# Opening a hybrid encoder layer with two column tiles interleaved, four tiles ahead of the first evacuation, and the gates' arithmetic spread among the matmuls

## The chip, the core and the metric

One NeuronCore of a Trainium2 chip runs the whole program in one launch. TensorE (PE, with its weight loads PEld), VectorE (DVE), ScalarE (ACT), GpSimd (POOL) and SyncE (SP, which only issues transfers here) each run their own queue in order and meet at semaphores. PE writes to PSUM, whose banks hold one 128x512 fp32 tile each; the other engines bring results from there to SBUF. The metric is the device time of one execution in microseconds, as the median of several runs.

## The reference

A layer on 512 tokens (two requests of 256) of width 2048, in fp32:

```python
xn = rmsnorm(h, norm_mix_w)
proj = xn @ w_in                       # 2048 x 7200
y_na = neighbourhood_attention(q, k, v, rpb)          # 8 heads of 128
qkv = silu(conv5(qkv)); q, k = l2norm(q), l2norm(k)   # 8 delta heads
beta = sigmoid(b)
g = -exp(A_log) * softplus(a + dt_bias)               # the gates
y_dn = delta_rule(q, k, v, g, beta) + flip(delta_rule(flipped ...))
h = h + concat(y_na, rmsnorm_and_silu_gate(y_dn, z)) @ w_out
h = h + (silu(rmsnorm(h) @ w_gate) * (rmsnorm(h) @ w_up)) @ w_down
y = rmsnorm(h, final_norm_w)
```

Within chunks of 64 tokens the delta rule needs the products k k^T and q k^T of each head (the "grams"), the running sum G of g, and the decays exp(G_c - G_s).

## The kernel before

Tokens lie along the free axis: x is held transposed, as 16 blocks (k-blocks) of 128 features by 512 tokens, and a *column tile* is 128 columns of `w_in` against all of them, accumulated in one PSUM bank. To keep fp32 precision every operand is split into a rounded high part and the rest (`split`, lines 134 to 142: ACT writes `hi`, DVE writes `lo`), and each k-block is three matmuls, hi hi, hi lo and lo hi (`mm3`). So a column tile is 48 matmuls. Its weights come in two halves of 512 KB (`load_w`), each from one of three SBUF buffers (`w_raw`, `w_hi`, `w_lo`); a buffer comes free when PE has used the half three before it.

The column tiles run in the order k0, q0, k1, q1, ... k7, q7 (key and query of each delta head), then the attention heads' q, k, v, then the rest. The RMS norm's per-token factor (`rstd`) isn't applied to x: each column tile is multiplied by it when it is evacuated from PSUM (`evac`, line 308). So the first evacuation waits for `token_rstd`: sixteen squares on ACT, their sum on DVE, a product with a matrix of ones on PE, a square root on ACT and four reciprocals on DVE.

The opening loads x and the two halves of k0 in quarters, in the order in which PE takes them (`load_k0`, `split_x`). Before its data are there, PE runs `WARM` products of a constant. After k0 come the 32 narrow products `ps_ba` for the gates' inputs a and b, then q0, the first half of k1, the ones product, the second half of k1, then q1. The column tiles take the three banks of the pool `pg` in turn; smaller products take the three banks of `psm` (`ps_s`).

For a delta head, `conv_silu` evacuates a tile (`ev_xi`), multiplies it with the five taps of the convolution (one on ACT, four on DVE, `cacc`), and applies silu on ACT into `kq`. Then ACT squares q (`q_sq`) and splits the squares (`sqh`, `sql`). `kq_post`, here called the head's post, makes the grams: eight gram products into two banks of `ps_s`, two products of the squares into the third, then copies by ACT (`gs`, line 380; `qrow`, line 388) and transfers by POOL. It runs as a generator: while PE's program is written, `pump` is called after every two k-blocks of a half tile (four times per half tile, eight per column tile), and each call advances the oldest post in `chains` and the oldest generator in `side` by one step. The first post fires at pump 21 (`KQ_START`), each later one 8 pumps after the post before it, or after it was put in the queue, whichever is later (`KQ_GAP`).

`gates` reads a and b back from DRAM with sixteen small transfers by POOL and computes softplus, g, G, beta and their exponentials on small tiles, called once after head 0. From head 2 on, `decays` puts 22 exponentials per head on ACT, in program order with the head's other ACT work (`pin`). Apart from what is pinned a scheduler orders each engine's instructions by priority; the weights' splits are raised by `AHEAD`.

Of the kernel before, what the change touches and what calls it, by code (L numbers as in the profile page):

```python
# [18 lines left out]
P = 128  # L19
T = 512  # L20
# [35 lines left out]
FIN_GAP = 5  # L56

LANE_WORK = 1800
OPEN_AT = 0
HALF, BAND = 32, 40  # L60

WARM = 56

DECAY_HEAD = 2
DECAY_ROWS = 11
# [2 lines left out]
def r32(ap):  # L68
    return ap.bitcast(F32)
# [3 lines left out]
def hybrid_encoder(ctx: ExitStack, tc: tile.TileContext, xT, w_in, w_ba, w_out, w_gate,  # L73
# [163 lines left out]
    def sm_tile():  # L237
        return psm.tile([P, T], F32, tag="s", name="ps_s")
# [8 lines left out]
    ba_raw = wp.tile([P, KT, 32], F32, tag="raw", bufs=3, name="ba_raw")  # L247
    baw = ini.tile([P, KT, 32], F32, tag="baw", name="ba_w")
    k0w = []

    def split_x(j):
        for i in range(2):
            k = 2 * j + i
            x, w = xr[j][:, i], nwm[:, k:k + 1]
            pin(act(out=xs[k][0], in_=x, func=AF.Copy, scale=w))
            stt(xs[k][1], x, w, r32(xs[k][0]), ALU.mult, ALU.subtract)  # L256


    ps = sm_tile()
# [2 lines left out]
        mm(ps[:, :2 * P], idle[:, :P], idle, start=True, stop=True)  # L262


    def load_k0(i, k):
        if k == 0:
            k0w.append((wp.tile([P, 8, P], F32R, tag="hi", bufs=3, name="w_hi"),
                        wp.tile([P, 8, P], F32R, tag="lo", bufs=3, name="w_lo"),
                        wp.tile([P, 8, P], F32, tag="raw", bufs=3, name="w_raw")))
        hi, lo, raw = [t[:, k:k + 4] for t in k0w[i]]  # L270
        nc.sync.dma_start(raw, w_in[0, i][:, k:k + 4])
        pin(act(out=hi, in_=raw, func=AF.Copy))
        tt(lo, raw, r32(hi), ALU.subtract)

    def load_x(j, i):
        nc.sync.dma_start(xr[j][:, i], xT[j][:, i])

    load_k0(0, 0)
    for j in range(8):
        if j == 0:  # L280
            load_x(0, 0)
            load_x(0, 1)
        else:
            nc.sync.dma_start(xr[j], xT[j])
        split_x(j)
        if j == 0:
            load_k0(0, 4)
        if j in (2, 4):
            load_k0(1, 2 * j - 4)
        if j == 5:  # L290
            nc.sync.dma_start(ba_raw, w_ba)
    tt(baw, ba_raw, nwm[:, :, None].broadcast_to([P, KT, 32]), ALU.mult)

    def token_rstd():
        acc = ini.tile([P, T], F32, tag="acc", name="ssq_acc")
        for k in range(KT):
            sq = acc if k == 0 else ini.tile([P, T], F32, tag="sq", bufs=2, name="x_sq")
            pin(act(out=sq, in_=xr[k // 2][:, k % 2], func=AF.Square))
            if k:
                tt(acc, acc, sq, ALU.add)  # L300
# [103 lines left out]
    def vec(nm, w=C):  # L404
        return ln.tile([P, w], F32, tag=nm, name=nm)
# [3 lines left out]
    def gates():  # L409
        bl, al = vec("bl", 4 * C), vec("al", 4 * C)  # L410
        for d in range(2):
            for t, r in ((bl, d * 8), (al, 16 + d * 8)):
                for k in range(4):
                    p0 = d * 64 + k * 16
                    nc.gpsimd.dma_start(
                        t[p0:p0 + 16].rearrange("p (g t) -> p g t", g=4),
                        s_ba[:, r:r + 8].rearrange("g h (b c t) -> (h b) g c t", b=NB, c=4)[:, :, k])
        for t in (bl, al):
            tt(t[:, :2 * C], t[:, :2 * C], t[:, 2 * C:], ALU.add)
            tt(t[:, :C], t[:, :C], t[:, C:2 * C], ALU.add)  # L420
# [3 lines left out]
        ts(xa, al, lpar[:, 0:1], None, ALU.add)  # L424
# [4 lines left out]
        ts(z, e, 2.0, None, ALU.add)  # L429
        nc.vector.reciprocal(z, z)  # L430
        tt(z, z, e, ALU.mult)
        tt(z2, z, z, ALU.mult)
        ts(sp, z2, 1.0 / 17, 1.0 / 15, ALU.mult, ALU.add)
# [3 lines left out]
        stt(sp, sp, 2.0, z, ALU.mult, ALU.mult)  # L437
        stt(sp, xa, 0.0, sp, ALU.max, ALU.add)
        g = vec("g")
        ts(g, sp, ea, -1.0, ALU.mult, ALU.mult)  # L440

        on = vec("on")
        nc.vector.memset(on, 1.0)  # L443
        G, NG = vec("G"), vec("NG")
        nc.vector.tensor_tensor_scan(G[half[0]], on[half[0]], g[half[0]], 0.0, ALU.mult, ALU.add)
        nc.vector.tensor_tensor_scan(G[half[1], ::-1], on[half[1]], g[half[1], ::-1], 0.0,
                                     ALU.mult, ALU.add)
# [3 lines left out]
        nc.vector.tensor_copy(tot[half[1]], G[half[1], 0:1])  # L451

        beta = vec("beta")
# [12 lines left out]
        nc.gpsimd.memset(E, 0.0)  # L466
        gt.update(G=G, NG=NG, beta=beta, kd=kd, eg=eg, dg=dg, E=E)
# [119 lines left out]

    for h in range(H):
        kq = wk.tile([P, 2, T], F32, tag="kq", bufs=2, name="kq")
        if h == 1:  # L590
            half_gemm(ps_k1, w_in[2, 1], xs[8:], False, True)
        ps = (ps_k0, ps_k1)[h] if h < 2 else col_tile(w_in[2 * h], xs)
        conv_silu(ps, 8 + h, kq[:, 0])
        ps = ps_q0 if h == 0 else col_tile(w_in[2 * h + 1], xs)
        conv_silu(ps, h, kq[:, 1])
        sq = na.tile([P, T], F32, tag="qT", name="q_sq")
        pin(act(out=sq, in_=kq[:, 1], func=AF.Square))
# [813 lines left out]
```

## Time and profile before

| | us |
|---|---|
| median of 3 runs | 2282.72 (2281.67 to 2284.06) |
| profiled execution | 2278.2 |
| its span in the trace | 2276.4 |
| PE busy | 2246.1 |
| DVE busy | 1768.7 |
| ACT busy | 1060.1 |
| POOL busy | 237.8 |

The span is the time from the first to the last instruction of the profiled execution. PE busy counts the matmuls, whose ends overlap the next ones' starts, so how fast PE advances is better read from the distance between starts. A wait is named by the instruction that waits and the one that released it.

### The profile page before, as it was taken

The page shows a single profiled execution, that of the slowest core. Times are in us where ns is not written, and L with a number is a line of the kernel's source. Part 1 is how long each engine was busy: PE and PEld are TensorE (multiplying, and loading weights), DVE is VectorE, ACT ScalarE, POOL GpSimd, SP SyncE. Part 2 cuts the span into 40 slices and gives each one's busy share as a digit, 9 for nine tenths or more (in the row PEclk, how much of TensorE's full clock was granted, in tenths as well). Part 3 has the DMA queues.
Part 4 walks back from the last instruction along what each step waited for, and adds up shares of the span by engine and source line. Part 5 has one row for each costly group of instructions (what it writes and reads, how often), then busy time and mean ns, then how long its engine had stood idle before and what let it go on. Part 6 is the DMA issues. An engine that isn't in the chain of part 4 may idle for free.

```text
span 2276.4 us, 32532 instructions
## 1 busy us (share of the span) xinstructions
PE 2246.1 (99%) x12318; PEld 1918.4 (84%) x12318; DVE 1768.7 (78%) x2691; ACT 1060.1 (47%) x1637; POOL 237.8 (10%) x343
## 2 busy tenths in 40 slices
PE   9999999999999999999999999999999999999998
PEld 7887778888888888888888888888888878888887
DVE  7654699984556546898888888888888788898966
ACT  6777332323333425654444444444444454444435
POOL 2211100010000011111111110111100011011010
PEclk9999999999999999999999999999999999999999
DMA  5333422254333455677777777777777477667672
GB/s 203 128 124 128 132 94 96 95 134 143 107 103 102 185 176 173 214 196 208 199 199 198 199 215 198 211 200 204 201 197 191 149 200 201 177 191 212 177 204 84
DMA packets 112828, 383.95 MB, mean 169 GB/s; under 512 B 14080, under 2 KB 14416, under 8 KB 112416
## 3 DMA queue, kind: packets, MB, share of 16 engines
q1 hardware_dynamic: 77264, 267.17, 34.2%
q0 software_dynamic: 34256, 112.61, 23.3%
q8 instruction: 97, 1.59, 0.3%
q10 hardware_dynamic: 1152, 2.10, 0.2%
q14 instruction: 59, 0.48, 0.1%
HBM read 346.41 MB, written 35.41 MB: 168 GB/s over the span
## 4 chain that ended last, share of the span: by engine, by line
PE 80%; DVE 10%; ACT 4%; issue 3%; DMA 2%; POOL 0%; SPq 0%; DVEq 0%; ACTq 0%; POOLq 0%
PE ps_g L85 25%; PE ps_c L85 14%; PE ps_d L85 14%; PE ps_a L85 14%; PE ps_b L85 7%; PE ps_s L85 5%; DVE w_lo L137 2%; DVE W L566 2%; DVE prod L564 1%; ACT w_hi L136 1%; DVE cacc L352 1%; ACT E L473 1%; ACT E L475 1%; PE ps_o L85 1%; DMA kkq<-s_gram 1%
## 5 line engine op out<-in xcount | busy, mean ns | idle before, releaser
L85 PE MATMUL ps_g<-xhi,w_hi 128*128 128x512 f32 x896 | 358.1, 400 | 1.6 <-DVE on L443 1.4
L85 PE MATMUL ps_g<-xhi,w_lo 128*128 128x512 f32 x896 | 350.4, 391 | 3.1 <-DVE w_lo L137 3.1
L85 PE MATMUL ps_g<-xlo,w_hi 128*128 128x512 f32 x896 | 349.6, 390 | 0.5 <-DVE xlo L256 0.5
L137 DVE TENSOR_TENSOR w_lo<-w_raw,w_hi 128x1024 fp32r<-128x1024 f32 x166 | 202.6, 1222 | 137.0 <-ACT w_hi L136 136.3
L136 ACT ACTIVATE w_hi<-b 128x1024 fp32r<-128x1024 f32 (+1 forms) x180 | 185.7, 1032 | 236.4 <-issue 119.0
L136 ACT ACTIVATE w_hi<-w_raw 128x1024 fp32r<-128x1024 f32 x166 | 174.6, 1056 | 243.3 <-PE ps_g L85 197.2
L136 ACT ACTIVATE w_hi<-w_first 128x1024 fp32r<-128x1024 f32 (+1 forms) x180 | 185.3, 1029 | 186.4 <-PE ps_c L85 90.3
L137 DVE TENSOR_TENSOR w_lo<-w_first,w_hi 128x1024 fp32r<-128x1024 f32 (+1 forms) x180 | 213.7, 1187 | 65.0 <-ACT w_hi L136 58.7
L137 DVE TENSOR_TENSOR w_lo<-b,w_hi 128x1024 fp32r<-128x1024 f32 (+1 forms) x180 | 212.9, 1183 | 7.1 <-ACT w_hi L136 6.7
L85 PEld LDWEIGHTS ps_g<-xhi,w_lo 128*128 128x128 f32 x896 | 168.2, 188 | 41.5 <-DVE w_lo L137 5.7
L85 PEld LDWEIGHTS ps_g<-xhi,w_hi 128*128 128x128 f32 x896 | 168.4, 188 | 38.5 <-issue 4.5
L85 PEld LDWEIGHTS ps_g<-xlo,w_hi 128*128 128x128 f32 x896 | 168.4, 188 | 35.3 <-DVE xlo L256 1.7
L85 PE MATMUL ps_d<-xc,w_hi 128*128 128x512 f32 x704 | 175.1, 391 | 0.0
L85 PE MATMUL ps_c<-xc,w_hi 128*128 128x512 f32 x704 | 175.1, 391 | 0.0
L85 PE MATMUL ps_a<-xc,w_hi 128*128 128x512 f32 x696 | 173.1, 391 | 0.0
L85 PEld LDWEIGHTS ps_c<-xc,w_hi 128*128 128x128 f32 x704 | 129.4, 188 | 25.0
L85 PEld LDWEIGHTS ps_d<-xc,w_hi 128*128 128x128 f32 x704 | 129.3, 188 | 25.0
L85 PEld LDWEIGHTS ps_a<-xc,w_hi 128*128 128x128 f32 x696 | 127.9, 188 | 24.8
L136 ACT ACTIVATE w_hi<-w_second 128x1024 fp32r<-128x1024 f32 (+1 forms) x60 | 61.9, 1032 | 98.4 <-DVE ga L1107 50.2
L85 PE MATMUL ps_d<-xc,w_lo 128*128 128x256 f32 x704 | 98.5, 283 | 0.0
L85 PE MATMUL ps_c<-xc,w_lo 128*128 128x256 f32 x704 | 98.5, 283 | 0.0
L85 PE MATMUL ps_a<-xc,w_lo 128*128 128x256 f32 x696 | 97.4, 283 | 0.0
(373 smaller groups left out, 4198.1 us busy)
## 6 DMA issues: line engine op xcount, KB each, us to landing
w_raw<-in_w_in_dram SPq DMA_DIRECT2D x110, 512.0 KB, 3.3
b<-in_w_gate_dram SPq DMA_DIRECT2D x66, 512.0 KB, 4.3
b<-in_w_up_dram SPq DMA_DIRECT2D x66, 512.0 KB, 4.9
b<-in_w_group_dram SPq DMA_DIRECT2D x48, 448.0 KB, 4.0
w_raw<-in_w_out_dram SPq DMA_DIRECT2D x32, 512.0 KB, 3.5
w_raw<-in_w_down_dram SPq DMA_DIRECT2D x24, 512.0 KB, 3.3
w_second<-in_w_gate_dram SPq DMA_DIRECT2D x22, 512.0 KB, 6.6
w_first<-in_w_gate_dram SPq DMA_DIRECT2D x22, 512.0 KB, 4.4
```

Source lines behind the costliest of these rows:

```text
L85: pin(nc.tensor.matmul(*a, **k))
L136: act(out=hi, in_=src, func=AF.Copy)
L137: tt(lo, src, r32(hi), ALU.subtract)
L352: stt(a3[:, :, lo:hi], x3[:, :, lo + o:hi + o], cw[:, ct, j:j + 1], a3[:, :, lo:hi], ALU.mult, ALU.add)
L473: pin(act(out=E[half[0], s, s:], in_=G[half[0], s:], func=AF.Exp, bias=NG[half[0], s:s + 1]))
L475: pin(act(out=E[half[1], s, :s + 1], in_=G[half[1], :s + 1], func=AF.Exp, bias=NG[half[1], s:s + 1]))
L564: tt(pv, W[:, s0:s1, s0:c], kkq[:, c, 0, None, s0:c].broadcast_to([P, n, j]), ALU.mult)
L566: nc.vector.tensor_reduce(W[:, s0:s1, c], pv, AX.X, ALU.add)
```

## The change

The opening runs k0 and q0 together, block by block: for each k-block three matmuls of k0 and three of q0, while x and the weights of both arrive in quarters. (The second half of q0's weights and the raw weights for a and b get buffers of their own in the pool `ini`.) Then come `ps_ba`, both halves of k1, and q1, which takes a bank of `psm`. The ones product stands behind the first two k-blocks of q1 (`RSTD_AT`). So four column tiles are computed before k2, which is the first to need an evacuated bank. `WARM` is 36 instead of 56. The gates become a generator in `side`: it issues its transfers at once, starts its arithmetic 8 pumps later (`GATE_START`) and does it in parts, one per pump, with DVE's part pinned in program order; what is left of it is done before head 2's decays.

```diff
-WARM = 56
+RSTD_AT = 2
+GATE_START = 8
+WARM = 36
...
-    load_k0(0, 0)
-    for j in range(8):
-        if j == 0:
-            load_x(0, 0)
-            load_x(0, 1)
-        else:
-            nc.sync.dma_start(xr[j], xT[j])
-        split_x(j)
-        if j == 0:
-            load_k0(0, 4)
-        if j in (2, 4):
-            load_k0(1, 2 * j - 4)
-        if j == 5:
-            nc.sync.dma_start(ba_raw, w_ba)
+    for k in range(0, KT, 4):
+        load_first(0, k)
+        if k:
+            load_first(1, k)
+        for j in (k // 2, k // 2 + 1):
+            if j:
+                nc.sync.dma_start(xr[j], xT[j])
+            for i in range(2):
+                if not j:
+                    nc.sync.dma_start(xr[j][:, i], xT[j][:, i])
+                split_x(2 * j + i)
+                if j == 0 and i == 0:
+                    load_first(1, 0)
+    nc.sync.dma_start(ba_raw, w_ba)
...
-    ps_k0 = pg.tile([P, T], F32, tag="g", name="ps_g")
-    for j in range(8):
-        for k in (2 * j, 2 * j + 1):
-            wh, wl, _ = k0w[k // 8]
-            mm3(ps_k0, wh[:, k % 8], wl[:, k % 8], xs[k][0], xs[k][1], k == 0, k == KT - 1)
+    ps_k0, ps_q0 = [pg.tile([P, T], F32, tag="g", name="ps_g") for _ in range(2)]
+    for k in range(KT):
+        for c, ps in enumerate((ps_k0, ps_q0)):
+            wh, wl, _ = k0w[c, k // 8]
+            mm3(ps, wh[:, k % 8], wl[:, k % 8], xs[k][0], xs[k][1], k == 0, k == KT - 1)
     ba_gemm(range(16))
-    ps_q0 = col_tile(w_in[1], xs)
     ps_k1 = pg.tile([P, T], F32, tag="g", name="ps_g")
     half_gemm(ps_k1, w_in[2, 0], xs[:8], True, False)
-    token_rstd()
+    half_gemm(ps_k1, w_in[2, 1], xs[8:], False, True)
+    ps_q1 = sm_tile()
+    wh, wl = load_w(w_in[3, 0], [8, P])
+    for k in range(8):
+        if k == RSTD_AT:
+            token_rstd()
+        mm3(ps_q1, wh[:, k], wl[:, k], xs[k][0], xs[k][1], k == 0, False)
+    half_gemm(ps_q1, w_in[3, 1], xs[8:], False, True)
...
+        yield from pause(GATE_START)
         for t in (bl, al):
-            tt(t[:, :2 * C], t[:, :2 * C], t[:, 2 * C:], ALU.add)
+            pin(tt(t[:, :2 * C], t[:, :2 * C], t[:, 2 * C:], ALU.add))
...
         for n in (13, 11, 9, 7, 5, 3, 1):
-            tt(sp, sp, z2, ALU.mult)
-            ts(sp, sp, 1.0 / n, None, ALU.add)
+            if n % 4 == 1:
+                yield
+            pin(tt(sp, sp, z2, ALU.mult))
+            pin(ts(sp, sp, 1.0 / n, None, ALU.add))
...
         if h == 0:
-            gates()
+            side.append(gates())
+            advance(side)
         if h >= DECAY_HEAD:
+            while side:
+                advance(side)
```

Three places in the engines' queues. First PE at its opening, behind the products of the constant (ps_s_132). xhi0_104 and xlo0_106 are the first eight k-blocks of x, high and rest. Before, ps_g_251 is k0:

```order
L85 LDWEIGHTS ones_72
L85 MATMUL ps_s_132<-ones_72 128x256
L85 MATMUL ps_g_251<-xhi0_104,w_hi_189 128x512
L85 MATMUL ps_g_251<-xlo0_106,w_hi_189 128x512
L85 MATMUL ps_g_251<-xhi0_104,w_lo_190 128x512
```

After, ps_g_249 is k0 and ps_g_250 is q0:

```order
L87 LDWEIGHTS ones_72
L87 MATMUL ps_s_132<-ones_72 128x256
L87 MATMUL ps_g_249<-xhi0_104,w_hi_169 128x512
L87 MATMUL ps_g_249<-xlo0_106,w_hi_169 128x512
L87 MATMUL ps_g_249<-xhi0_104,w_lo_170 128x512
L87 MATMUL ps_g_250<-xhi0_104,w_hi_178 128x512
L87 MATMUL ps_g_250<-xlo0_106,w_hi_178 128x512
L87 MATMUL ps_g_250<-xhi0_104,w_lo_179 128x512
```

Each k-block of x now feeds six matmuls in a row instead of three. Second, PE around the ones product (<-ssq_acc). Before, ps_g_377 is k1 and ps_g_626 is q1, which takes k0's bank:

```order
L85 MATMUL ps_g_377<-xhi0_104,w_lo_381 128x512
L85 MATMUL ps_s_455<-ssq_acc_408,ones_72 128x512
L85 MATMUL ps_g_377<-xhi1_105,w_hi_588 128x512
...
L85 MATMUL ps_g_377<-xhi1_105,w_lo_589 128x512
L85 MATMUL ps_g_626<-xhi0_104,w_hi_629 128x512
```

After, ps_g_363 is k1, ps_s_424 is q1, and ps_g_628 is k2, which takes k0's bank:

```order
L87 MATMUL ps_g_363<-xhi1_105,w_lo_397 128x512
L87 MATMUL ps_s_424<-xhi0_104,w_hi_427 128x512
...
L87 MATMUL ps_s_484<-ssq_acc_437,ones_72 128x512
...
L87 MATMUL ps_s_424<-xhi1_105,w_lo_514 128x512
L87 MATMUL ps_g_628<-xhi0_104,w_hi_631 128x512
```

The ones product moved from the middle of k1 to behind the first six matmuls of q1; 42 matmuls instead of 24 follow it before k0's bank is taken again. Third, ACT at the end of head 2's share of decays (E), of which the last is shown. Before, ps_s_1011 and ps_s_1016 hold the grams of head 2:

```order
L136 ACTIVATE sqh_874<-q_sq_872 128x512
L473 ACT_TABLE_LOAD
...
L475 ACTIVATE E_582<-G_561,NG_562 64x11
L136 ACTIVATE w_hi_1127<-w_raw_1125 128x1024
L346 ACTIVATE cacc_990<-ev_xi_988,cw_89 128x512
L380 COPY gs_1024<-ps_s_1011 128x256
L380 COPY gs_1028<-ps_s_1016 128x256
```

After, ps_s_1002 and ps_s_1007 hold those of head 1, and head 2's post takes the same banks on PE 8 pumps behind head 1's:

```order
L138 ACTIVATE sqh_835<-q_sq_833 128x512
L484 ACT_TABLE_LOAD
...
L486 ACTIVATE E_815<-G_788,NG_789 64x11
L361 ACT_TABLE_LOAD
L361 ACTIVATE kq_862<-cacc_951 128x2x128 x2
L385 COPY gs_1015<-ps_s_1002 128x256
L385 COPY gs_1019<-ps_s_1007 128x256
```

So head 1's copies moved from ahead of these decays to behind them, and the split and the cacc that stood between moved ahead. From the next share of decays on, the order on every engine is the old one.

More of the change, by code (lines that the diff above doesn't have):

```diff
@@ L246, in hybrid_encoder, with split_x @@
     xr = [ini.tile([P, 2, T], F32, tag=f"xr{j}", name="x_raw") for j in range(8)]
-    ba_raw = wp.tile([P, KT, 32], F32, tag="raw", bufs=3, name="ba_raw")
+    ba_raw = ini.tile([P, KT, 32], F32, tag="bar", name="ba_raw")
     baw = ini.tile([P, KT, 32], F32, tag="baw", name="ba_w")
[L249 to L256, printed above, removed]
+    k0w = {}
+    def split_x(k):
+        x, w = xr[k // 2][:, k % 2], nwm[:, k:k + 1]
+        pin(act(out=xs[k][0], in_=x, func=AF.Copy, scale=w))
+        stt(xs[k][1], x, w, r32(xs[k][0]), ALU.mult, ALU.subtract)
     ps = sm_tile()
@@ L262, in hybrid_encoder, with load_first @@
         mm(ps[:, :2 * P], idle[:, :P], idle, start=True, stop=True)
[L265 to L271, printed above, removed]
+    def load_first(c, k):
+        if k % 8 == 0:
+            pool, bufs = (ini, 1) if (c, k) == (1, 8) else (wp, 3)
+            k0w[c, k // 8] = [pool.tile([P, 8, P], dt, tag=tag, bufs=bufs, name="w_" + tag)
+                              for tag, dt in (("hi", F32R), ("lo", F32R), ("raw", F32))]
+        hi, lo, raw = [t[:, k % 8:k % 8 + 4] for t in k0w[c, k // 8]]
+        nc.sync.dma_start(raw, w_in[c, k // 8][:, k % 8:k % 8 + 4])
         pin(act(out=hi, in_=raw, func=AF.Copy))
         tt(lo, raw, r32(hi), ALU.subtract)
-    def load_x(j, i):
-        nc.sync.dma_start(xr[j][:, i], xT[j][:, i])
-    load_k0(0, 0)
-    for j in range(8):
-        if j == 0:
-            load_x(0, 0)
-            load_x(0, 1)
-        else:
-            nc.sync.dma_start(xr[j], xT[j])
-        split_x(j)
-        if j == 0:
-            load_k0(0, 4)
-        if j in (2, 4):
-            load_k0(1, 2 * j - 4)
-        if j == 5:
-            nc.sync.dma_start(ba_raw, w_ba)
+    for k in range(0, KT, 4):
[12 more added lines that the diff above has]
+    nc.sync.dma_start(ba_raw, w_ba)
     tt(baw, ba_raw, nwm[:, :, None].broadcast_to([P, KT, 32]), ALU.mult)
@@ L417, in gates @@
                         s_ba[:, r:r + 8].rearrange("g h (b c t) -> (h b) g c t", b=NB, c=4)[:, :, k])
+        yield from pause(GATE_START)
         for t in (bl, al):
-            tt(t[:, :2 * C], t[:, :2 * C], t[:, 2 * C:], ALU.add)
-            tt(t[:, :C], t[:, :C], t[:, C:2 * C], ALU.add)
+            pin(tt(t[:, :2 * C], t[:, :2 * C], t[:, 2 * C:], ALU.add))
+            pin(tt(t[:, :C], t[:, :C], t[:, C:2 * C], ALU.add))
         bl, al = bl[:, :C], al[:, :C]
         xa, ax, e, z, z2, sp = vec("xa"), vec("ax"), vec("e"), vec("z"), vec("z2"), vec("sp")
-        ts(xa, al, lpar[:, 0:1], None, ALU.add)
+        pin(ts(xa, al, lpar[:, 0:1], None, ALU.add))
         act(out=ax, in_=xa, func=AF.Abs)
@@ L428, in gates @@
         act(out=ea, in_=lpar[:, 1:2], func=AF.Exp)
[L429 to L433, printed above, removed]
-        for n in (13, 11, 9, 7, 5, 3, 1):
-            tt(sp, sp, z2, ALU.mult)
-            ts(sp, sp, 1.0 / n, None, ALU.add)
-        stt(sp, sp, 2.0, z, ALU.mult, ALU.mult)
-        stt(sp, xa, 0.0, sp, ALU.max, ALU.add)
+        yield
+        pin(ts(z, e, 2.0, None, ALU.add))
+        pin(nc.vector.reciprocal(z, z))
+        pin(tt(z, z, e, ALU.mult))
+        pin(tt(z2, z, z, ALU.mult))
+        pin(ts(sp, z2, 1.0 / 17, 1.0 / 15, ALU.mult, ALU.add))
+        for n in (13, 11, 9, 7, 5, 3, 1):
+            if n % 4 == 1:
+                yield
+            pin(tt(sp, sp, z2, ALU.mult))
+            pin(ts(sp, sp, 1.0 / n, None, ALU.add))
+        yield
+        pin(stt(sp, sp, 2.0, z, ALU.mult, ALU.mult))
+        pin(stt(sp, xa, 0.0, sp, ALU.max, ALU.add))
         g = vec("g")
-        ts(g, sp, ea, -1.0, ALU.mult, ALU.mult)
+        pin(ts(g, sp, ea, -1.0, ALU.mult, ALU.mult))
         on = vec("on")
```

5 lines of the change are left out of this document (2 added, 3 removed).

## The prediction

> **What bounds the kernel now.** I read the page first, then who waits for whom on PE, then PE's order of time in the first 125 us, then ACT's and DVE's at the places where PE is fed.
>
> The page's head and PE's longest waits (waiter <- releaser: us in total, times, longest):
>
> ```profile
> span 2276.4 us, 32532 instructions
> PE 2246.1 (99%) x12318; PEld 1918.4 (84%) x12318; DVE 1768.7 (78%) x2691; ACT 1060.1 (47%) x1637; POOL 237.8 (10%) x343
> PE ps_g L85 <- DVE w_lo L137: 3.9, 6, 1.1
> PE ps_g L85 <- DVE on L443: 1.4, 1, 1.4
> ```
>
> PE is the bound everywhere. An edit pays only where PE idles, does work that produces nothing, or is fed late; the change reaches only the first 150 us. PE there (start, duration, instruction, and in brackets idle time before it), and one undisturbed stretch from the chain:
>
> ```profile
> 1.06 8.70 PE L85 MATMUL ps_s<-ones 128*128 128x256 bf16 x56 [1.06 <-DVE epsc L108]
> 9.52 0.48 PE L85 MATMUL ps_g<-xhi,w_hi 128*128 128x512 f32 x1
> 17.40 0.50 PE L85 MATMUL ps_g<-xlo,w_hi 128*128 128x512 f32 x1 [0.19 <-DVE xlo L256]
> 22.10 3.64 PE L85 MATMUL ps_ba<-x_raw,ba_w 128*32 128x512 f32 x32
> 42.17 1.02 PE L85 MATMUL ps_s<-ssq_acc,ones 128*128 128x512 f32 x2
> 42.63 0.79 PE L85 MATMUL ps_g<-xhi,w_hi 128*128 128x512 f32 x1
> 43.26 0.40 PE L85 MATMUL ps_g<-xlo,w_hi 128*128 128x512 f32 x1
> 50.08 0.47 PE L85 MATMUL ps_g<-xhi,w_hi 128*128 128x512 f32 x1 [1.44 <-DVE on L443]
> 802.81 70.79 PE ps_g L85 x312
> ```
>
> The last row gives the step of a 128x512 matmul: 70.79 / 312 = 0.227 us. A half tile is 24 of them, 5.44 us; a column tile 10.9 us.
>
> **Term 1, fewer warm-up products.** Stretches of 1 us (PE and PEld busy and counts are the columns that matter):
>
> ```profile
> 3.00:4.00 1.00, 1.00 (x6) 0.71 (x5) 0.00 (x0) 0.14 (x1) 1.00 (x3) 1.00 0.30 90
> 7.00:8.00 1.00, 1.00 (x12) 0.90 (x10) 1.00 (x2) 0.41 (x1) 0.00 (x0) 1.00 1.02 388
> 8.00:9.00 1.00, 1.00 (x12) 0.90 (x10) 0.15 (x1) 0.00 (x0) 0.00 (x0) 1.00 1.03 384
> ```
>
> Five weight loads per us early, ten later: a warm-up product costs 0.20 us, then 0.10. The twenty that go are late ones: 20 x 0.10 = 2.0, and the first real matmul can start at 9.52 - 2.0 = about 7.5. It finds its input: rows of term 2. **-2.0.** [...]
>
> **Term 2, input in step.** ACT and DVE on the first inputs, and DMA over 10 us (last column GB/s):
>
> ```profile
> 9.33 2.60 ACT L255 ACTIVATE xhi<-x_raw,nwm 128x512 fp32r<-128x512 f32 x4 [1.92 <-DMA x_raw<-in_xT_dram]
> 11.83 0.61 ACT L272 ACTIVATE w_hi<-w_raw 128x512 fp32r<-128x512 f32 x1
> 10.09 2.74 DVE L256 SCALAR_TENSOR_TENSOR xlo<-x_raw,nwm,xhi 128x512 fp32r<-128x512 f32 x4 [1.94 <-ACT xhi L255]
> 12.74 0.69 DVE L273 TENSOR_TENSOR w_lo<-w_raw,w_hi 128x512 fp32r<-128x512 f32 x1
> 10.00:20.00 10.00, 9.52 (x39) 6.66 (x39) 9.91 (x16) 9.20 (x16) 0.00 (x0) 1.00 1.03 406
> ```
>
> Before, 48 matmuls take 22.10 - 9.52 = 12.58 instead of 10.90: 1.7 is lost to late xlo. Now four k-blocks need 4 x 262 KB of x and 2 x 262 KB of weights, 1.57 MB, 3.9 us at 406 GB/s; ACT 4 x 0.65 + 2 x 0.61 = 3.8, DVE 6 x 0.69 = 4.1; PE spends 24 x 0.227 = 5.4. So the engines that feed it gain on it. Only the third block is late: as many bytes stand ahead of its x on SP's queue as before, so xhi at 9.33, xlo ready at 10.09 + 0.7 = 10.8, and PE is there at 7.5 + 13 x 0.227 = 10.45. I count 0.5 lost in place of 1.7. The raw weights of a and b now come last on SP's queue, behind 6.3 MB in all: some 16 us at that rate, so near 21, and ba needs them at 7.5 + 21.8 + 0.5 = 29.8. **-1.2** (bounds -1.7 and 0).
>
> **Term 3, the first evacuation.** Before, the q1 tile needs the bank of k0, and so rstd, one half tile after the ones product. Without waits PE would be there at 42.17 + 0.46 + 5.44 = 48.07; it starts at 50.08, 2.0 late (0.46 is 42.63 - 42.17). 0.4 of that is the slow matmul behind the ones product (43.26 - 42.63 against 0.23), which stays. **-1.6** (bounds -2.0 and 0), if the new cover holds. By the order on PE, 42 matmuls instead of 24 now stand between the ones product and the bank's next use, and six of q1 ahead of it.
>
> ```profile
> 25.40 0.61 ACT L298 ACTIVATE ssq_acc<-x_raw 128x512 f32<-128x512 f32 x1
> 37.81 1.05 ACT L136 ACTIVATE w_hi<-w_raw 128x1024 fp32r<-128x1024 f32 x1
> 40.03 0.69 DVE L300 TENSOR_TENSOR ssq_acc<-ssq_acc,x_sq 128x512 f32<-128x512 f32 x1
> 49.25 0.68 DVE L308 TENSOR_TENSOR ev_xi<-ps_g,rstd 128x512 f32<-128x512 f32 x1
> ```
>
> The new wait: on ACT the split of q1's first weights now waits for PE's last block of k0 (it takes that tile's buffer), and all sixteen squares queue behind it. From there: split 1.05, then squares and sums, 40.72 - 25.40 = 15.3 before with two splits among them, some 14.1 with one: 15.2. PE needs 3 x 0.227 + 3.6 (ba) + 54 x 0.227 = 16.5. 1.3 us of cover; each us beyond it costs one. Then product to k0's evacuation, 49.93 - 42.17 = 7.8, against 0.46 + 42 x 0.227 = 10.0 on PE: 2.2 of cover. The gates' input follows ba, so POOL's write and sixteen reads start about 2 us later; the first sum, which DVE now holds in its place, comes only behind three evacuations, three tiles' taps and four splits. Should the reads land after that, DVE stands, with q1's evacuation and the next w_lo behind the sum; nothing in the trace puts them so late, and I count it at nothing.
>
> **Term 4, what is late next.** The gates' arithmetic itself is the same count of instructions on DVE, which has gaps, and costs PE nothing. But four tiles wait for evacuation at once, and the pumps that fire each head's gram products (its post) are now counted from k2 on, no longer from the second half of k1. ACT, with decays of head 2 (22 exponentials) and the gram copies:
>
> ```profile
> 92.33 0.73 ACT L356 ACTIVATE kq<-cacc 128x256 f32<-128x256 f32 x2
> 92.96 1.04 ACT L136 ACTIVATE w_hi<-w_raw 128x1024 fp32r<-128x1024 f32 x1
> 93.91 0.62 ACT L597 ACTIVATE q_sq<-kq 128x512 f32<-128x512 f32 x1
> 94.56 0.63 ACT L136 ACTIVATE sqh<-q_sq 128x512 fp32r<-128x512 f32 x1
> 95.21 1.28 ACT L473 ACT_TABLE_LOAD   x1
> 96.50 0.35 ACT L473 ACTIVATE E<-G,NG 64x64 f32<-64x64 f32 x1
> 103.82 1.06 ACT L136 ACTIVATE w_hi<-w_raw 128x1024 fp32r<-128x1024 f32 x1
> 104.78 0.71 ACT L346 ACTIVATE cacc<-ev_xi,cw 128x512 f32<-128x512 f32 x1
> 105.40 0.63 ACT L380 COPY gs<-ps_s 128x256 f32<-128x256 f32 x2
> 85.89 1.09 PE L85 MATMUL ps_s<-kq 128*64 128x128 f32 x16
> 98.36 1.09 PE L85 MATMUL ps_s<-kq 128*64 128x128 f32 x16
> 121.71 1.09 PE L85 MATMUL ps_s<-kq 128*64 128x128 f32 x16
> 138.60 3.10 DVE L352 SCALAR_TENSOR_TENSOR cacc<-ev_xi,cw,cacc 128x508 f32<-128x508 f32 x4
> ```
>
> By the order on ACT the copies behind these decays are now head 1's, before head 2's, and head 2's grams come not 23.4 us after (121.71 - 98.36) but 8 pumps, 12.5 us (98.36 - 85.89), as head 1's to head 2's before. They need the same three banks of ps_s, so PE waits for the copies. Count both sides from PE's end of tile k3, at which ACT may split k4's first half. PE: 78 matmuls and one post (12.47 - 48 x 0.227 = 1.6): 19.3. ACT and DVE: split 0.95, its w_lo 1.2, four taps of q2 3.1, table 1.3, silu 0.65, split 0.95, q_sq 0.65, cacc 0.62, sqh 0.65, table and decays 103.82 - 95.21 = 8.6, table 1.3, silu 0.65, copy 0.3: 20.9; with some eight hand-overs between engines, and up to 0.9 in which ACT is still busy with the gates' exponentials, 21 to 22.7. **+2.5** (bounds +1.7 and +3.4). This is a tail of 4-tile backlog: behind it the order on all engines is the old one, so nothing is handed on.
>
> **Sum.** -2.0 - 1.2 - 1.6 + 2.5 = -2.3. The profiled execution took 2278.2 with its span of 2276.4; the median of the runs is 2282.72, 4.5 higher. So span 2274.1, its execution 2275.9, median **2280.4**. With the bounds of term 4 and a few tenths on term 2 the forecast's own range is 2278 to 2282.
>
> **Rivals.** *The copies are in time*: term 4 is nothing, -4.8, 2277.9. For it: ACT is 47% busy over the span. Against it: in the rows of term 4, from 92.33 to 106, it has no gap, and the count above is a chain in which each step needs the one before. *The gates come late* (the other side): eg, kd and el on ACT wait for G and tot, and head 0's row copies and k4's split queue behind them in order. In the trace xa to G takes 17 us:
>
> ```profile
> 70.77 0.16 DVE L424 TENSOR_SCALAR xa<-al,lpar 128x64 f32<-128x64 f32 x1
> 87.99 0.29 DVE L446 TENSOR_TENSOR_SCAN G<-on,g 64x64 f32<-64x64 f32 x1
> ```
>
> I place G near 88 again, just ahead of ACT's need. Each us later adds one to term 4; from 2.3 the kernel is slower, with 4 it takes 2282.7 - 4.8 + 6.5 = 2284.4. *It is not fed*: if the doubled weight stream delays x by 2 us, terms 1 and 2 are gone: -1.6 + 2.5, 2283.6. Against it stand the 5.4 us against 4.1 of term 2.
>
> **Chances.** Forecast 0.60, copies in time 0.20, gates late 0.12, not fed 0.08. About 0.2% (4.6 us) is what a measurement of this kernel can tell from no change: below 2278.2 lie most of the first rival (0.16) and the forecast's lower edge (0.09), above 2287.3 the tails of the last two (0.07). The range runs from all gains and a slightly larger term 1, 2277.2, to the late gates, 2284.5.
>
> **What would show it.** First real matmul near 7.5; ba done by 29.8 + 3.6 = 33.4; no idle on PE at k2, which starts at 33.4 + 21.8 + 0.9 = 56.1; an idle of 2 to 3 us on a gram product, released by ACT's copy, three column tiles, a post and 19.3 us behind that, near 110. It is wrong if PE idles before the ones product, if that idle is absent, or if later stretches change.

## The result and the profile after

The changed kernel took a median of 2276.57 us (2273.99 to 2278.42, 10 runs) beside 2281.12 us (2277.35 to 2284.06, 10 runs) of the kernel before: ratio 0.9982, 95% interval 0.9973 to 0.9990, 4.55 us faster. Two repeats gave 0.9980 (0.9971 to 0.9989) each. The forecast was 2280.4, or 2.3 us faster, and its range began at 2277.2. The profiled execution took 2274.4 us with its span of 2272.6 (forecast 2275.9 and 2274.1).

The page's head, and PE's row from the list of waits (waiter <- releaser: us in total, times, longest):

```profile
span 2272.6 us, 32505 instructions
PE 2245.3 (99%) x12298; PEld 1919.5 (84%) x12298; DVE 1768.9 (78%) x2693; ACT 1057.8 (47%) x1637; POOL 237.1 (10%) x343
PE ps_s L87 <- ACT gs L385: 1.5, 1, 1.5
```

PE in order of time (start, duration, instruction, idle before it):

```profile
1.06 6.66 PE L87 MATMUL ps_s<-ones 128*128 128x256 bf16 x36 [1.06 <-DVE epsc L110]
7.48 0.48 PE L87 MATMUL ps_g<-xhi,w_hi 128*128 128x512 f32 x1
11.06 0.50 PE L87 MATMUL ps_g<-xlo,w_hi 128*128 128x512 f32 x1 [0.29 <-DVE xlo L257]
30.16 3.64 PE L87 MATMUL ps_ba<-x_raw,ba_w 128*32 128x512 f32 x32
46.11 1.02 PE L87 MATMUL ps_s<-ssq_acc,ones 128*128 128x512 f32 x2
85.15 1.09 PE L87 MATMUL ps_s<-kq 128*64 128x128 f32 x16
111.69 1.09 PE L87 MATMUL ps_s<-kq 128*64 128x128 f32 x16 [1.52 <-ACT gs L385]
142.12 1.09 PE L87 MATMUL ps_s<-kq 128*64 128x128 f32 x16
390.54 1.32 PE L87 MATMUL ps_s<-kT,qT 128*128 128x160 f32 x8 [0.78 <-DVE W L577]
```

The first real matmul stands at 7.48 (forecast 7.5; 6.84 and 7.12 in the other two profiles of the changed kernel, so a match this close is luck), only the third k-block waits, ba ends at 33.8 (33.4), the 1.44 us at q1's bank is gone, and the new wait for ACT's gram copy stands where it was forecast (near 110), but with 1.52 us. ACT and DVE beside it:

```profile
90.71 1.06 ACT L138 ACTIVATE w_hi<-w_raw 128x1024 fp32r<-128x1024 f32 x1 [0.20 <-PE ps_g L87]
109.36 1.28 ACT L361 ACT_TABLE_LOAD   x1
110.66 0.72 ACT L361 ACTIVATE kq<-cacc 128x256 f32<-128x256 f32 x2
111.28 0.63 ACT L385 COPY gs<-ps_s 128x256 f32<-128x256 f32 x2
```

```profile
42.24 2.28 DVE L299 TENSOR_TENSOR ssq_acc<-ssq_acc,x_sq 128x512 f32<-128x512 f32 x3
51.92 0.68 DVE L307 TENSOR_TENSOR ev_xi<-ps_g,rstd 128x512 f32<-128x512 f32 x1
```

The squares are summed at 44.52, so the cover ahead of the ones product (46.11) is 1.6 us; k0 is evacuated by 52.6, ahead of k2.

Against the kernel before, at the same instructions (means over four profiles of before and three of after, all of unchanged copies; "W" is the product behind W, "xc" the one that waits for xc near 950):

| place | before (spread) | after (spread) | difference |
|---|---|---|---|
| gram products of head 4 | 145.15 (144.86 to 145.41) | 141.91 (141.72 to 142.12) | -3.24 |
| gram products of head 7 | 216.25 (215.95 to 216.48) | 213.62 (213.45 to 213.81) | -2.63 |
| W | 393.98 (393.16 to 394.48) | 390.39 (390.04 to 390.59) | -3.6 |
| xc | 953.7 (951.93 to 955.75) | 949.5 (949.33 to 949.69) | -4.2 |
| span | 2278.1 (2276.4 to 2280.5) | 2272.8 (2272.6 to 2273.2) | -5.3 |

So 3.2 us are gained by head 4, 0.6 is given back by head 7, and the rest appears in code that the change doesn't touch, where before alone spreads by up to 4 us. What is given back shows as waits of PE for the split squares of q, 0.98 us in sum from head 5 to head 7 in the first profile of before and 1.44 in the first of the changed kernel. The largest is head 6's; before, then after:

```profile
193.17 0.40 PE L85 MATMUL ps_s<-sqh,ones_r 128*1 128x512 f32 x1 [0.17 <-ACT sqh L136]
190.84 0.40 PE L87 MATMUL ps_s<-sqh,ones_r 128*1 128x512 f32 x1 [0.45 <-ACT sqh L138]
```

### The profile page after: what moved, and what is told of

It reads as the page before. It is cut to its first block, busy times and chain, and to the rows that moved or that the text cites. A ratio compares the mean times of both kernels' runs of the same rounds, so it can differ in the third digit from the quotient of the medians.

```text
span 2272.6 us, 32505 instructions
## 1 busy us (share of the span) xinstructions
PE 2245.3 (99%) x12298; PEld 1919.5 (84%) x12298; DVE 1768.9 (78%) x2693; ACT 1057.8 (47%) x1637; POOL 237.1 (10%) x343
## 4 chain that ended last, share of the span: by engine, by line
PE 81%; DVE 9%; ACT 4%; issue 2%; DMA 2%; POOL 0%; SPq 0%; DVEq 0%; ACTq 0%; POOLq 0%
PE ps_g L87 25%; PE ps_d L87 14%; PE ps_c L87 14%; PE ps_a L87 14%; PE ps_b L87 7%; PE ps_s L87 6%; DVE w_lo L139 2%; DVE W L577 2%; DVE prod L575 2%; DVE cacc L357 1%; ACT w_hi L138 1%; ACT E L484 1%; ACT E L486 1%; DMA w_first<-in_w_group_dram 1%; PE ps_o L87 1%
## 5 line engine op out<-in xcount | busy, mean ns | idle before, releaser
L87 PE MATMUL ps_g<-xhi,w_hi 128*128 128x512 f32 x880 | 352.0, 400 | 0.0
L87 PE MATMUL ps_g<-xhi,w_lo 128*128 128x512 f32 x880 | 344.3, 391 | 2.0 <-DVE w_lo L139 2.0
L87 PE MATMUL ps_g<-xlo,w_hi 128*128 128x512 f32 x880 | 343.8, 391 | 0.3 <-DVE xlo L257 0.3
```

The lines of the kernel that those rows point to most:

```text
L87: pin(nc.tensor.matmul(*a, **k))
```

## The experiments

All were timed in five rounds, each together with the kernel before. "Gain" is that kernel's median minus the tried one's; brackets hold the ratio and its 95% interval.

### The opening, one part undone at a time

**e1 and e14: 56 warm-up products in the changed kernel.**

```
-WARM = 36
+WARM = 56
```

> The changed kernel with 56 warm-up products instead of 36, all else as changed. If term 1 is right, the first real matmul starts at 9.5 instead of 7.48, the input is then well ahead (the 0.29 us wait at the third k-block goes), the gram products of head 4 and the end come 1.7 to 2.0 us later: ratio to before about +0.08% worse than that of the changed kernel. If the opening is fed by the input anyway, the first matmul is later but ba and the ones product stay within 0.5 us of 30.16 and 46.11, and the time is that of the changed kernel.

> The changed kernel with 56 warm-up products, a second time: the first run's median was 3.2 us above the changed kernel's, its trace only 1.85 us later at the last gram copies (224.95 against 222.93 to 223.30). If warm-up is worth what the traces show, the median is 1.5 to 2.2 above the changed kernel's 2275.5; if it is worth more than the opening shows, 3 or more again.

PE in e1:

```profile
9.80 0.48 PE L87 MATMUL ps_g<-xhi,w_hi 128*128 128x512 f32 x1
47.74 1.02 PE L87 MATMUL ps_s<-ssq_acc,ones 128*128 128x512 f32 x2
```

The ones product comes at 47.74 and 47.82 instead of 45.92 (mean of 46.11, 45.76, 45.88): 1.9 us, and so do head 7's gram products (215.47, 215.52). Gains: 1.51 and 0.66 us, ratios 0.9995 (0.9987 to 1.0004) and 0.9996 (0.9987 to 1.0005), where the changed kernel has 0.9980 to 0.9982. So the times give the twenty products some 3 to 4 us, the traces of the opening 1.9. In the two profiles W comes 2.0 us later in the mean, xc 3.1 and 6.0: what is beyond 1.9 appears behind W, in code that the edit doesn't touch.

**e10 and e13: 36 warm-up products in the kernel before**, the same edit the other way.

> The kernel before with 36 warm-up products instead of 56 and nothing else changed: term 1 alone. If the warm-up is on the path, all 2.0 us come off (ones product at 40.2, span 2274.4). If the opening of before is bound by its input, as the run with the one-tile opening suggests (first matmul at 7.33 but ba at 21.75, against 9.52 and 22.10), the ones product stands at 41.8 to 42.2 and the time is that of the kernel before.

> The kernel before with 36 warm-up products, a second time: in the first run the median was 2.6 us below the kernel before while the one profile was no faster (ones product at 42.90 against 41.96 to 42.42, its x landing late, xhi at 10.10 against 9.18 to 9.60). If the profile was an execution with late input, this one has its ones product at 40.5 to 41.5 and the median is 1.5 to 2.6 lower again. If the opening of before is bound by its input, the product stands at 41.8 or later and the median comes within 1 us of the kernel before.

PE in e13, whose first matmul is at 7.66:

```profile
9.72 0.49 PE L85 MATMUL ps_g<-xhi,w_hi 128*128 128x512 f32 x1 [0.41 <-ACT xhi L255]
10.50 0.50 PE L85 MATMUL ps_g<-xlo,w_hi 128*128 128x512 f32 x1 [0.29 <-DVE xlo L256]
41.77 1.02 PE L85 MATMUL ps_s<-ssq_acc,ones 128*128 128x512 f32 x2
```

In the traces term 1 alone gains next to nothing: PE waits for x, and the ones product stands at 41.77 in e13 and at 42.90 in e10 (where the clock, behind a wait of 1.95 us for x, fell to 0.50 at 12.8 us) beside 41.96 to 42.55. Yet both medians fell, by 2.62 and 2.27 us (0.9991, 0.9982 to 0.9999; 0.9988, 0.9979 to 0.9997). A profile is one execution and the timed ones leave no trace; why they gain more stays open.

**e6: one tile in the opening.** The input code and the k0 loop as before; 36 products, four tiles ahead and the gates in parts stay.

```
-    for k in range(KT):
-        for c, ps in enumerate((ps_k0, ps_q0)):
-            wh, wl, _ = k0w[c, k // 8]
-            mm3(ps, ...)
+    for j in range(8):
+        for k in (2 * j, 2 * j + 1):
+            wh, wl, _ = k0w[k // 8]
+            mm3(ps_k0, ...)
     ba_gemm(range(16))
+    ps_q0 = col_tile(w_in[1], xs)
```

> The changed kernel, but with the input's loads and the first column tile written as before (k0 alone in step with the input, then ba, then q0, k1, q1); 36 warm-up products, four tiles ahead and the gates in parts stay. If term 2 is right, the 1.2 us that two tiles in step save come back as waits for xlo ahead of ba, and because the start is 2 us earlier than before, the input is late by more: ones product between 47.3 and 49.2 instead of 46.1, the end 1.2 to 3.1 us later. [...]

PE and ACT in e6:

```profile
52.64 1.12 PE L87 MATMUL ps_s<-ssq_acc,ones 128*128 128x512 f32 x2 [3.86 <-DVE ssq_acc L302]
```

```profile
36.35 1.06 ACT L138 ACTIVATE w_hi<-w_raw 128x1024 fp32r<-128x1024 f32 x1 [4.38 <-PE ps_g L87]
37.31 0.61 ACT L300 ACTIVATE ssq_acc<-x_raw 128x512 f32<-128x512 f32 x1
```

Without the wait the product would stand at 52.64 - 3.86 = 48.8, 2.9 later than in the changed kernel: what the joint opening is worth beside the earlier start. The wait itself nobody had counted: on ACT the splits of the next weights wait for PE to free buffers, the squares queue behind the last of them (36.35), and the sum is late. Head 7's products come 8.1 us later; the median is 4.95 us above before (ratio 1.0022, 1.0013 to 1.0031).

**e7: three tiles ahead.** The sum of squares stands between the halves of k1, q1 in a bank of ps_g, as before; the rest as changed.

```
     half_gemm(ps_k1, w_in[2, 0], xs[:8], True, False)
-    half_gemm(ps_k1, w_in[2, 1], xs[8:], False, True)
-    ps_q1 = sm_tile()
-    ...
+    token_rstd()
...
```

> The changed kernel, but the sum of squares and rstd stand between the two halves of k1 as before and q1 takes a bank of ps_g behind k0's evacuation: three tiles ahead of the first evacuation instead of four. The opening in step and the gates in parts stay. If term 3 is right, PE waits 1.4 to 2.0 us at q1's first matmul for k0's evacuation; if term 4 is right (the backlog of a fourth tile is what makes the gram products of head 2 wait), the 1.5 us at 111.69 goes. Together -0.1 to +0.5, the end at 2272.5 to 2273.1. If term 3 was worth nothing here, no wait and 1.5 us faster; if the wait for the gram copies has another cause than the fourth tile, it stays and the kernel is 1.6 slower.

PE in e7, and stretches of 1 us (PE busy, its count, then PEld, DVE, ACT, POOL, the granted clock, DMA share, GB/s):

```profile
42.96 2.07 PE L87 MATMUL ps_s<-ssq_acc,ones 128*128 128x512 f32 x2 [3.51 <-DVE ssq_acc L299]
45.26 0.63 PE L87 MATMUL ps_g<-xlo,w_hi 128*128 128x512 f32 x1
103.14 0.39 PE L87 MATMUL ps_s<-sqh,ones_r 128*1 128x512 f32 x1 [0.92 <-ACT sqh L138]
```

```profile
39.00:40.00 1.00, 0.46 (x3) 0.03 (x1) 0.90 (x2) 0.84 (x2) 1.00 (x1) 1.00 0.00 0
41.00:42.00 1.00, 0.00 (x0) 0.00 (x0) 0.95 (x2) 0.98 (x3) 0.29 (x1) 0.77 0.00 0
45.00:46.00 1.00, 1.00 (x4) 0.81 (x3) 0.21 (x1) 0.91 (x2) 0.00 (x0) 0.50 0.03 8
48.00:49.00 1.00, 1.00 (x5) 0.77 (x4) 1.00 (x2) 0.00 (x0) 0.00 (x0) 0.82 0.00 0
49.00:50.00 1.00, 1.00 (x6) 0.82 (x5) 0.97 (x3) 0.00 (x0) 0.00 (x0) 1.00 0.00 0
```

The wait for head 1's copies went, as the theory of term 4 says, but head 2's products now wait for k, q and the split squares instead, 0.83, 0.92 (the last PE row above) and 0.48 us. And the cover of the ones product went too: with two tiles in step ba starts at 30, so do the last splits ahead of the squares, and one half tile doesn't cover the sums. PE idles 3.51 us, and the clock pays once more: granted at 0.50 from 41.5 to 48.4, matmuls 0.43 us apart instead of 0.23, (48.4 - 43.0) / 2 = 2.7 us. The wait at q1's bank that was expected never showed, since the first evacuation had time in that stretch. Median 1.50 us above before (1.0005, 0.9996 to 1.0013); against the changed kernel timed with it 5.8.

**e3 and e17: the gates in one piece in the changed kernel, unpinned.** e3's edit also left out three of the seven multiplications by z2 in the series; e17 is the edit whole.

```
-        yield from pause(GATE_START)
-            pin(tt(t[:, :2 * C], t[:, :2 * C], t[:, 2 * C:], ALU.add))
+            tt(t[:, :2 * C], t[:, :2 * C], t[:, 2 * C:], ALU.add)
...
-            side.append(gates())
-            advance(side)
+            gates()
```

> The changed kernel with the gates' arithmetic unpinned and issued in one piece where head 0 ends, as before. If the edit on the gates is free (costed at nothing in the forecast), the gram products of heads 1 to 4 start within 0.3 us of the changed kernel's (85.15, 97.62, 111.69) and the time is the same. If laying the gates out in parts is what the gain comes from, a wait of PE for a w_lo behind gate instructions on DVE, like the 1.44 us one of before, comes back and the end is 1 to 3 us later. If the late gates delay the decays, head 2's grams come earlier here, by up to 1.5 us.

> The changed kernel with the gates' function as in the kernel before, all of its arithmetic in one piece where head 0 ends and unpinned (e3's edit had also left out three of the seven multiplications by z2 in the series, 0.7 us of VectorE). If what cost there was VectorE's order (the gates ahead of the third evacuation), it comes again and a little larger: PE idle 5.3 to 6.5 us near 83 on ev_xi, then 6.8 or 3.4 us at clock 0.50, last gram copies 8 us or more behind the changed kernel's 223.1, median 7 to 9 us above it. If the missing multiplications had shifted the order, the idle is gone and the time is the changed kernel's.

PE and DVE in e17:

```profile
84.05 0.77 PE L87 MATMUL ps_g<-xhi,w_hi 128*128 128x512 f32 x1 [6.06 <-DVE ev_xi L307]
```

```profile
74.82 0.55 DVE L435 RECIPROCAL z<-z 128x64 f32<-128x64 f32 x1
83.02 0.29 DVE L469 TENSOR_SCALAR dg<-ident,el 128x128 f32<-128x128 f32 x1
83.22 0.68 DVE L307 TENSOR_TENSOR ev_xi<-ps_g,rstd 128x512 f32<-128x512 f32 x1
```

Left to the scheduler, the whole series runs ahead of k1's evacuation, PE's next tile waits 6.06 us for the bank (5.29 in e3), and 6.8 us at clock 0.50 follow. The edit takes away three things at once, the delay, the parts and the pinning; no run separates them. Medians 4.71 us (1.0021, 1.0012 to 1.0030) and 2.59 us (1.0014, 1.0005 to 1.0023) above before.

**e18: the gates in parts in the kernel before**, nothing else of the change.

```
+GATE_START = 8
...
-            gates()
+            side.append(gates())
+            advance(side)
```

> The kernel before with the gates in parts and pinned, and nothing else of the change. If the forecast's zero for this edit holds where only three tiles are ahead, the gram products stand within 0.3 us of before's (98.2 to 98.7 for the third, 121.5 to 122.1 for the fourth) and the time is the same. If it is worth something by itself, the 1.44 us wait at q1's first matmul or the waits behind 190 shrink and it is 0.5 to 1.5 us faster.

PE in e18:

```profile
99.28 0.96 PE L86 MATMUL ps_s<-kq 128*64 128x128 f32 x12 [0.87 <-ACT kq L357]
101.38 0.59 PE L86 MATMUL ps_s<-sqh,ones_r 128*1 128x512 f32 x1 [0.92 <-ACT sqh L137]
102.24 0.59 PE L86 MATMUL ps_s<-sql,ones_r 128*1 128x512 f32 x1 [0.28 <-DVE sql L138]
```

Alone the edit costs: head 2's k and q come late on ACT, PE waits three times, the clock drops to 0.50 for 3.4 us, and the median is 2.49 us above before (1.0012, 1.0003 to 1.0021). So each part undone takes most or all of the gain. Of the parts alone, the warm-up was seen to gain, by 2.6 and 2.3 us in the times, and the gates to cost; the joint opening and the fourth tile were not tried alone.

### The wait for the gram copies

**e2: head 2's products four pumps later.**

```
-        yield from pause(KQ_START if h == 0 else KQ_GAP)
+        yield from pause({0: KQ_START, 2: 12}.get(h, KQ_GAP))
```

> The changed kernel with the gram products of head 2 alone held back four pumps more (12 instead of 8). If the 1.5 us idle at 111.69 is PE waiting for ACT's copies of head 1 behind the decays (term 4), the idle goes and every gram product from head 4 on comes 1.5 us earlier: span 2271.1. If ACT's backlog itself is the limit, the wait turns up at the next user of ACT's work (a weight split, or head 3's gram products), and the span stays at 2272.6 within 0.4.

```profile
132.07 0.59 PE L87 MATMUL ps_s<-sqh,ones_r 128*1 128x512 f32 x1 [3.46 <-ACT qrow L393]
```

The wait only moved, to head 3 (its row on PE above), and grew. Gain 4.94 us (0.9979, 0.9970 to 0.9989): the changed kernel's. That is odd at first, since head 7's products stand at 216.04, level with the kernel before. But ACT copies them at 224.35, 1.1 to 1.6 us ahead of its place there, and W comes at 391.22 (before 393.16 to 394.48): PE's place at head 7 is not what carries the gain.

**e8: KQ_START 16; e9: KQ_START 16 and head 3 four pumps later.**

```
+        yield from pause({0: 16, 3: 12}.get(h, KQ_GAP))
```

> The changed kernel with the first head's gram products four pumps earlier (16 instead of 20), so that head 1's copies stand ahead of head 2's exponentials on ACT, as they did before the change. The run that held head 2's products back moved the wait to head 3's (3.5 us at 132). If the wait of term 4 is the copies of one head caught behind the exponentials of the next with only 12.5 us between their products, both waits go here, no gram product waits for ACT by more than 0.5 us, and head 4 on comes 1.5 us earlier: span about 1.5 below that of the changed kernel. If ACT's work itself is too much for the stretch, a wait of about 1.5 us shows again on some product of heads 1 to 3 and nothing is gained.

> The changed kernel with the gram products of head 0 four pumps earlier (16 instead of 20) and those of head 3 four pumps later than the run before (12 instead of 8), so they stand 6.125, 7.125, 8.125 and 9.625 column tiles into the program where the changed kernel has 6.625, 7.625, 8.625 and 9.625. Head 1's copies then come ahead of head 2's exponentials and head 3's k and q are ready. If term 4's wait is a matter of order on ACT, no gram product of heads 0 to 3 waits by more than 0.3 us, the clock stays at 1.00 and head 4's stand 1.5 us earlier than in the changed kernel (near 140.4): span 1.5 lower. If ACT's work is too much for the stretch in any order, one of them waits 1 us or more and nothing is gained.

PE in e8, then in e9:

```profile
117.48 1.18 PE L87 MATMUL ps_s<-kq 128*64 128x128 f32 x16 [0.97 <-ACT kq L361]
120.38 0.39 PE L87 MATMUL ps_s<-sqh,ones_r 128*1 128x512 f32 x1 [1.72 <-ACT sqh L138]
```

```profile
165.78 0.40 PE L87 MATMUL ps_s<-sqh,ones_r 128*1 128x512 f32 x1 [1.07 <-ACT sqh L138]
```

e8 trades the wait for head 3's own k and q. In e9 no gram product of heads 0 to 3 waits, and head 4's stand at 140.21, 1.7 earlier: term 4's wait is a matter of order on ACT. But 1.07 us come back at head 5, head 7's products stand 0.65 earlier (212.97), and the time is the changed kernel's (2275.34 beside 2275.50, timed together; 0.9977, 0.9968 to 0.9986): by then PE waits for ACT whatever the order at heads 0 to 3. e8 has 0.9977 too (0.9969 to 0.9986). Neither beats the changed kernel by what can be told apart.

**e15: e9 with 16 warm-up products**, a try for more.

```
+WARM = 16
```

> The changed kernel with the gram products spread as in e9 and only 16 warm-up products: a try for a faster version. If the input sets the opening, PE starts near 4.3 but waits for x, the ones product stands at 45.2 to 45.9 and the time is that of the changed kernel within 1 us. If PE's idle time while it waits keeps the clock low, matmuls of 0.43 us appear after 5 us and the ones product comes later than 46.5. If the warm-up is on the path, ones product at 44 to 45 and 1 to 2 us faster.

```profile
6.23 0.51 PE L87 MATMUL ps_g<-xhi,w_hi 128*128 128x512 f32 x1 [1.58 <-ACT xhi L256]
46.36 1.02 PE L87 MATMUL ps_s<-ssq_acc,ones 128*128 128x512 f32 x2
```

A stretch of 1 us, columns as in e7:

```profile
9.00:10.00 1.00, 1.00 (x4) 0.80 (x3) 0.09 (x1) 0.84 (x2) 0.00 (x0) 0.50 1.10 434
```

PE waits for x at once, the granted clock is 0.50 from 8.1 to 11.5 us, and the ones product comes at 46.36, no better than with 36. Gain 3.75 us (0.9980, 0.9971 to 0.9989).

### Where the rest of the gain lies

**e4, e11, e16: before again; e5, e12: after again**, unchanged copies.

> The kernel before, unchanged, for a second profile of it. The changed kernel gained 2.5 us by 950 us and 3.7 by the end; the other 1.2 lies in the lead blocks of the two down groups (waits for split weights near 1856 to 1866 and 2041 to 2048: 3.6 and 1.5 us before, 1.8 and 1.1 after). If that part varies from execution to execution, this profile has these waits different by 0.5 us or more while the gram products of heads 1 to 7 stand within 0.2 us of 85.89, 98.36, 121.71, 145.06. If it belongs to the kernel, the waits come out as 3.6 and 1.5 again within 0.3.

> The changed kernel, unchanged, for a second profile of it. Two profiles of the kernel before differ by 1.1 us at 802 us from one weight split near 252, and by 1.7 to 0 us in waits near 1860. If the opening alone is the gain, this profile has its gram products at 85.15 to 213.81 within 0.7 us, and more waiting near 1850 to 1866 than the 1.8 us of the first profile (2.5 to 3.5), so that from 951 us on it gains nothing on the kernel before: span 2273 to 2274.5. If the later gain belongs to the change, the 1.8 us come again and the span is 2272.6 within 0.5.

> The kernel before, unchanged, for a third profile. In its first two, from the matmul that waits for xc (near 952) to the last product (near 2267) it took 1314.5 and 1314.4 us, and the waits of the two down groups were 6.5 and 5.0 us; other kernels with the same code there took 1313.3 to 1314.7 and waited 2.9 to 5.1. If the 0.8 us that the changed kernel gained there is scatter, this one falls within 1313.3 to 1314.7; if it belongs to the change, it is 1314.4 or more again.

> The changed kernel, unchanged, for a third profile. Its first two took 1313.3 and 1314.0 us from the matmul that waits for xc to the last product, and had the last gram products at 213.8 and 213.5 (before: 216.2 and 216.4). If only the opening is gained, these come at 213.2 to 214.1 again and the later stretch anywhere from 1313.3 to 1314.7; if the later gain belongs to the change, 1314.0 or less.

> The kernel before, unchanged, for a fourth profile: from ACT's copies of the last head's gram products to the products that wait for W the three profiles so far took 167.5, 168.6 and 168.9 us, the changed kernel 167.2, 167.7 and 167.0 with the same code. If the round trip through memory in this stretch is scatter alone, this one may lie anywhere from 166.4 to 168.9; at 168 or more it speaks for a part of the gain of 1 us that belongs to the change.

Before against itself gave 0.9998 (0.9989 to 1.0007), 1.0003 (0.9994 to 1.0011) and 1.0000 (0.9991 to 1.0009). From xc to the last products before took 1314.3 to 1314.8 us in its four profiles, the changed kernel 1313.3, 1314.0 and 1314.2: of the 1.2 us that the first two traces showed there, 0.7 is left in the means. With all runs, the seven profiles of before and its variants took 1314.3 to 1315.6, the thirteen of the changed kernel and its variants 1313.0 to 1314.7. The means are 0.8 apart, and most of it arises in waits for split weights near 1860, where the code is equal. Scatter alone may not make that; whether it belongs to the change stays open. Between head 7 and W the traces name the path. ACT in the kernel before, then in the changed one: the copy of head 7's gram products, and the last quarter of the grams, read back from memory.

```profile
225.63 0.63 ACT L380 COPY gs<-ps_s 128x256 f32<-128x256 f32 x2
247.28 1.91 ACT L490 COPY kkq<-kkq 64x2048 f32<-64x2048 f32 x1 [1.86 <-DMA kkq<-s_gram]
```

```profile
223.30 0.63 ACT L385 COPY gs<-ps_s 128x256 f32<-128x256 f32 x2
244.67 1.90 ACT L501 COPY kkq<-kkq 64x2048 f32<-64x2048 f32 x1 [0.64 <-DMA kkq<-s_gram]
```

The product behind W follows that fourth copy by 145.87 us (390.54 - 244.67), in before by 145.88, and by 145.8 to 145.9 in every profile where the two were compared, whether PE's clock fell on the way or not. So from ACT's copy for head 7 to 390 us PE, 99% busy, isn't the bound: a chain is, that starts at this copy and goes through memory (e2 shows the same). That round trip makes the copy-to-W time 167.5, 168.6, 168.9 and 168.0 us in before, 167.2, 167.7 and 167.0 in after, 166.4 to 168.9 over all kernels. The means differ by 0.96, but the ranges overlap, and e16's 168.0 stands on the line drawn for it: how much of it belongs to the change stays open. Behind W a wait of PE for ACT's dvn near 540 ran up to 3.48 us in equal code (0.52 to 2.43 in before, 3.48 in e14), which makes most of the spread at xc.

## Why the prediction was wrong, step by step

- **Terms 1 and 2 held in their sum, and term 3 in what is left.** Thirty matmuls more (30 x 0.227 = 6.81) now stand ahead of the ones product; it moved from 42.28 to 45.92, so terms 1 and 2 gave 3.64 - 6.81 = -3.2 (forecast -2.0 - 1.2). Head 4 shows -3.24; with the 1.5 of term 4 taken out that is -4.8, which leaves -1.6 for term 3, as forecast. But they aren't separate: term 1 alone is lost to the input in the traces (e10, e13), and terms 2 and 3 undone singly cost far more than their price (e6, e7).
- **Term 4 is the term that was mis-sized**: cause, place and order were right, 2.5 was 1.5, below its own lower bound of 1.7. PE took 19.7 us from k3's end (90.5) to the products against 19.3 counted, the ACT chain 21.2 against "21 to 22.7". So 0.4 of the 1.0 is PE's side, and 0.6 is the chain, whose low end held where I took the middle, mostly for hand-overs.
- **"Nothing is handed on" failed, and with it "PE is the bound everywhere".** Waits for ACT give 0.6 us of the gain back between heads 4 and 7, and from there a chain through memory sets the pace, not PE. The forecast carried -2.3 unchanged to the end; its own sign of being wrong, "if later stretches change", is what came.
- **The gates at nothing**: right in the whole change, but for another reason than given. "DVE has gaps" isn't enough: unpinned, the same instructions cost PE 6 us (e17), and alone they cost 2.5 us (e18). It is their place that makes them free.
- **The anchor**: 2282.72 was a median of three runs; of ten, with these three among them, it was 2281.12, and 2279.7 to 2281.3 when timed later. Of the 3.8 us by which the forecast missed, 1.6 is this: from 2281.12 the same working gives 2278.8 and a range that begins at 2275.6, below the 2276.57 measured. 1.0 is term 4. The remaining 1.2 is not settled: a warm-up worth more in the times than in traces, the round trip, or the stretch near 1860.
- **Rivals**: "the copies are in time" comes nearest with 2277.9, but not by its mechanism, since the copies were late. "Gates late" did not come (G at 88, as placed), nor "not fed".

## What to carry to other kernels

Price a wait in two parts: its length, and what the clock takes afterwards: here no lone wait of up to 1.52 us lowered it, waits of 1.6 to 2.5 did in some profiles and not in others, and each one of 3.46 or more did. Edits that re-time one stretch come as a set: cover, buffers and engine order of one hold up the other, and undoing one doesn't show its price. An engine at 99% may still not be the bound: look for an instruction that follows another by the same time in every profile (here by 145.8 to 145.9 us). Anchor on more than three runs.

## What the runs showed of the hardware

**The clock after a wait.** The 1.52 us wait of the changed kernel left it at 1.00. Idles of 3.46 (e2), 3.48 (e14), 3.51 (e7), 3.86 (e6), 5.29 (e3) and 6.06 us (e17) each brought 0.50, and so did e8's and e18's three shorter waits within 4 us; e7's three of 0.83, 0.92 and 0.48 did not. The slow stretches behind these lasted 6.8 us (e2, e3, e7, e17) or 3.4 us (e6, e8, e14, e18), nothing between; the drop came 1.9 us after PE fell idle in e2 and, in e6, over 1 us after PE was at work again. With idles between 1.52 and 3.46 us both came: every one of the twenty profiles has a wait of 1.9 us for kT that ends between 273 and 284 us, and by 284 us seven of them have fallen to 0.50 behind it, for 3.4 us in the five whose stretch ends by then; what decides it was not shown. In the first and the second profile of the changed kernel, in stretches of 1 us:

```profile
277.00:278.00 1.00, 1.00 (x3) 0.76 (x3) 0.83 (x6) 0.00 (x0) 0.00 (x0) 0.50 0.82 303
```

```profile
277.00:278.00 1.00, 1.00 (x6) 0.83 (x5) 0.83 (x7) 0.00 (x0) 0.00 (x0) 1.00 0.80 270
```

Each such fall (near 277, 540 and 1860 in code that no kernel changed) takes up to 1.7 us from PE, an estimate: half of 3.4, since behind the fall in the first of these profiles the matmuls stand 0.43 us apart instead of 0.23. It can be part of the spread between runs of one kernel. Near 277 the fall didn't reach W, which came at 390.54 us with the fall and at 390.59 without it in these two profiles.

**The start of PE.** Behind the same 36 warm-up products the first real matmul stood between 6.33 and 7.66 us. In the kernels that keep the joint opening, the fourth tile and 36 products it stood between 6.44 and 7.48, the ones product between 45.41 and 46.11, so waits for the input take up a part of the spread, 1.04 us at the first and 0.70 at the second.
